# Hybrid decoder layer on one Trainium2 core: the opening's load order, cast order and count of warm-up products

## The chip, the core and the metric

The kernel runs on one core of one Trainium2 chip. The core has a matmul engine (TensorE, in the profile PE for products and PEld for weight loads), a vector engine (VectorE, DVE), a scalar engine (ScalarE, ACT), a general engine (GpSimd, POOL) and a synchronisation engine (SyncE, SP). Transfers between HBM and on-chip memory (DMAs) are issued by SP, ACT and POOL, each into a queue of its own, and move on sixteen shared DMA engines. The metric is the time of one execution on the device in microseconds (us); lower is better.

## The reference

One layer is computed for two groups of rows with shared weights: 1024 prompt rows and 64 sample rows (8 requests of 8 tokens), 1088 rows of width 1024 in all.

```python
xn = rmsnorm(x, norm1_g)
proj = xn @ w_in
q, k, v, glu_a, glu_b, gate_a, gate_b = jnp.split(proj, SPLIT_IDX, axis=-1)
...
branch_a = attn @ w_o_attn
u = glu_a * jax.nn.sigmoid(glu_b)
...
c = dwconv_valid(u_ext, conv_b_w, conv_b_bias)
branch_b = jax.nn.silu(layernorm(c, ln_b_g, ln_b_b)) @ w_pb
merged = jax.nn.sigmoid(gate_a) * branch_a + jax.nn.sigmoid(gate_b) * branch_b
h = x + merged @ w_out
up = rmsnorm(h, norm2_g) @ w_up
...
y = h + (jax.nn.silu(gate) * val) @ w_down
```

The change touches only the start of the first two lines: the norm of `x` and its product with the first pieces of `w_in`.

## The kernel before

**How a product is made.** The activations are kept transposed, channels on the partitions. Each f32 matrix is split in two: a rounded high part (a cast on ACT) and the low rest (a subtraction on DVE). `mm3` then runs three products for each 128-channel slice k: high activations with high weights (L197), low activations with high weights (L198), high activations with low weights (L199). A weight piece is 128 output channels by 1024 input channels; its 1024 columns are eight slices.

**Chunks.** The 1088 rows are taken in three chunks of 384, 384 and 320 (`CHUNKS`). `stream_side` (SIDES) runs several weight pieces side by side in a chunk: for chunk 0 the first three pieces, slice by slice, then pieces four and five one after the other; for chunk 1 two pieces side by side, then the others. So chunk 0 is 3 x 24 products for the side pieces (tiles `whi`/`wlo` twice and `whix`/`wlox`), 24 for the fourth (`whiy`/`wloy`) and 24 for the fifth (in the spare tiles `q`). Chunk 1 starts behind them with the pairs into the `aux` banks.

**The opening.** PE first runs 12 warm-up products of the tile `mean` with itself (L662); their result is not used. `norm1_load` issues the loads of chunk 0: `x_part` for slices of the rows (tile `xr`), `w_part` for columns of the three first weight pieces (tiles `wraw`, `wraw` and `u`; columns 0 to 255, 256 to 511, 512 to 1023). SP's queue takes piece one and the rows; the first and second parts of pieces two and three go through ACT's queue and POOL's. Behind those ACT loads its table and runs one small operation (`warm`, L851).

`norm1_raw` then makes the parts for chunk 0 without waiting for the norm: for each slice k, ACT scales the rows by the gain into `xh` (L283), DVE makes `xl` (L284). The weight pieces are cast in four parts of 256 columns (`W_PARTS`, two slices each), L178 on ACT and L179 on DVE. Each output row is corrected later by its own factor 1/rms, which is a column scale of the transposed output.

**The norm factors.** The squares of chunk 0 are summed by `norm1_chain` (L310 on ACT, L312 on DVE, low priority), those of chunk 1 by `norm1_squares` (L296, L294). A product with `mean` sums over the partitions (`norm1_factor`, L322), ACT takes the root (L326, tile `rows`), DVE the reciprocal and its parts (L327 to L329), six products spread the factor over the partitions (`spread`, L340), ACT copies it (L348, tile `rstd`). Chunk 1 is multiplied by its factor before its products: DVE L356 (`xr`), ACT L357 (`xh`), DVE L358 (`xl`). So chunk 1's products wait for chunk 1's factor.

**What sets the order.** Each engine runs its instructions in the order in which the program holds them. That order is made when the program is built: a scheduler takes the instructions by priority, with its own model of when each would be ready. `issue_after(x)` holds the next instruction behind x in that order; `later(...)` lowers a priority. An instruction that the scheduler thinks ready earlier can therefore be put in another place on every engine, though its line of source has not moved.

Of the kernel before, what the change touches and what calls it, by code (L numbers as in the profile page):

```python
# [8 lines left out]
AF = mybir.ActivationFunctionType  # L9
# [71 lines left out]
SQUARES_LATER = 3000  # L81
W_PARTS = 4
CONV_LATER = 1200
LN_AT = ((0, 1, 17, 36), (2, 37, 50, 80), (60, 81, 103, 134), (90, 135, 152, 183))
# [43 lines left out]
class Build:  # L128
    def __init__(self, tc, a):
        self.tc, self.nc, self.a = tc, tc.nc, a  # L130
        self.order, self.groups, self.n_in = weight_order()
        self.uid = 0
        self.agenda, self.now = [], 0

    @contextmanager
# [107 lines left out]
    def norm1_load(self, pp, c):  # L243
        o, n = CHUNKS[c]
        xr = self.t(pp, [P, KT, n], f"xr{c}")
        load = self.nc.sync.dma_start
# [10 lines left out]
        def w_part(i, x, load=load):  # L257
            z = slice(*ends[x:x + 2])
            load(self.w_raw[i][:, z], self.a["wall"][i][:, z])

        w_part(0, 0)
        x_part(0, 1)
        for x in range(2):
            for i in (1, 2):
                w_part(i, x, (self.nc.scalar, self.nc.gpsimd)[x].dma_start)
        x_part(1, 2)
# [8 lines left out]
    def norm1_raw(self, c, xr, xh, xl):  # L275
        parts = list(zip(*[self.w_parts(W_PARTS) for _ in range(SIDE)]))
        for k in range(KT):
            part = parts[k * W_PARTS // KT] if k * W_PARTS % KT == 0 else ()
            early = len(part) if k else 1
            for p in part[:early]:  # L280
                p()
            h = xh[c][:, k, :]
            self.nc.scalar.activation(h, xr[:, k, :], AF.Identity, scale=self.c("g1", k))  # L283
            self.nc.vector.scalar_tensor_tensor(xl[c][:, k, :], xr[:, k, :], self.c("g1", k), h.bitcast(F32),  # L284
                                                ALU.mult, ALU.subtract)
            for p in part[early:]:
                p()
# [340 lines left out]
    def run(self):  # L628
        nc, tc, a = self.nc, self.tc, self.a
        es = ExitStack()  # L630
        with es:
# [28 lines left out]
            ps = self.bank("mm")  # L660
            for _ in range(12):
                nc.tensor.matmul(ps[:, 0:P], self.mean, self.mean, start=True, stop=True)  # L662
# [16 lines left out]
    def phase_x(self):  # L679
# [170 lines left out]
        raw, xr[0] = self.norm1_load(p0, 0)  # L850
        nc.scalar.activation(self.warm, self.warm, AF.Sqrt)  # L851
        self.w_load()
# [1314 lines left out]
```

## Time and profile before

| what | value |
|---|---|
| time, median of 3 runs | 1641.81 us (1641.48 to 1642.1) |
| the profiled execution's own time | 1641.73 us |
| its span, first to last instruction | 1639.9 us |
| outside the span | 1.83 us |
| PE busy | 1631.1 us |
| DVE, ACT, POOL busy | 1401.3, 880.5, 262.7 us |
| bytes moved by DMA | 201.58 MB, mean 123 GB/s |

Times in the profile are microseconds from the start of the span, except where ns stands. A row of the timeline gives the start, the time taken, the engine, the line, the operation, output and input tiles (numbers of buffers left out) and how many instructions were merged; in square brackets how long the engine had been idle and what ended that. A matmul is pipelined, so the time of a row is longer than the distance to the next start; the distance between starts is what PE needs for one. Each warm-up product and each other product of plain f32 tiles stands as two records, so 12 warm-up products are 24.

### The profile page before, as it was taken

Reading aid. Unit: us, or ns where it says so; the run is one execution under the profiler, and the core shown is the slowest. Engines: PE = TensorE matmul, PEld = TensorE weight load, DVE = VectorE, ACT = ScalarE, POOL = GpSimd, SP = SyncE. Lnnn points to the kernel's source line nnn. Section 1 sums busy time; section 2 is a strip of 40 time slices with the busy share of each in tenths; the row PEclk is TensorE's granted clock in tenths of the full one; section 3 lists DMA queues with packets and bytes.
Section 4 is the critical chain, followed back from the end, with each engine's and each line's share of the span. In section 5 each row is a group of like instructions: output and inputs, shape, how many; then the busy total and the mean of one; then the engine's idle time right before and its main releaser. Section 6 shows DMA issues by size and latency. Waiting matters only on the chain.

```text
span 1639.9 us, 30209 instructions
## 1 busy us (share of the span) xinstructions
PE 1631.1 (99%) x11540; PEld 1615.2 (98%) x11540; DVE 1401.3 (85%) x2597; ACT 880.5 (54%) x1845; POOL 262.7 (16%) x549
## 2 busy tenths in 40 slices
PE   9999999999999999999999999999999999999998
PEld 9999999999999999999999999999999999999997
DVE  7899979999979996788755999988888887989867
ACT  6524277774488754676532465555555555524322
POOL 0100111222011201111102422222222111000000
PEclk9999999999999999999999999999999999999999
DMA  6221222323121356548763631344444334765413
GB/s 211 85 60 52 64 74 57 107 83 114 43 70 42 89 183 195 172 164 224 188 226 107 212 119 66 111 119 115 115 117 117 99 113 145 252 163 161 110 62 110
DMA packets 104857, 201.58 MB, mean 123 GB/s; under 512 B 25992, under 2 KB 56712, under 8 KB 104696
## 3 DMA queue, kind: packets, MB, share of 16 engines
q1 hardware_dynamic: 81384, 131.34, 26.5%
q0 software_dynamic: 22752, 67.79, 13.8%
q8 instruction: 90, 1.47, 0.4%
q10 hardware_dynamic: 576, 0.53, 0.1%
q14 instruction: 55, 0.45, 0.1%
HBM read 137.55 MB, written 64.03 MB: 123 GB/s over the span
## 4 chain that ended last, share of the span: by engine, by line
PE 87%; DVE 7%; ACT 3%; DMA 2%; issue 1%; ACTq 0%; SPq 0%; DVEq 0%; POOLq 0%
PE mm L197 20%; PE mm L198 20%; PE mm L199 20%; PE aux L199 6%; PE aux L198 6%; PE aux L197 6%; PE aux L417 1%; DVE c L531 1%; ACT ct L611 1%; PE aux L429 1%; PE aux L430 1%; PE aux L407 1%; PE aux L408 1%; DVE bt L531 1%; DMA ct<-d_c 1%
## 5 line engine op out<-in xcount | busy, mean ns | idle before, releaser
L197 PE MATMUL mm<-xh,whi 128*128 128x384 f32 (+1 forms) x904 | 301.3, 333 | 0.0
L199 PE MATMUL mm<-xh,wlo 128*128 128x384 f32 (+1 forms) x904 | 295.4, 327 | 0.0
L198 PE MATMUL mm<-xl,whi 128*128 128x384 f32 (+1 forms) x904 | 295.2, 327 | 0.1
L198 PEld LDWEIGHTS mm<-xl,whi 128*128 128x128 f32 x904 | 170.0, 188 | 1.2 <-DVE xl L284 0.4
L197 PEld LDWEIGHTS mm<-xh,whi 128*128 128x128 f32 x904 | 169.9, 188 | 0.7
L199 PEld LDWEIGHTS mm<-xh,wlo 128*128 128x128 f32 x904 | 169.7, 188 | 0.1
L1414 DVE SCALAR_TENSOR_TENSOR acc<-st,fc,acc 128x1104 f32<-128x1104 f32 x88 | 119.7, 1363 | 12.2 <-issue 6.7
L178 ACT CAST whi<-wraw 128x1024 fp32r<-128x1024 f32 (+1 forms) x62 | 59.5, 966 | 66.2 <-PE mm L198 51.7
L199 PE MATMUL mm<-th,wlo 128*128 128x272 f32 x320 | 92.4, 289 | 0.0
L197 PE MATMUL mm<-th,wlo 128*128 128x272 f32 x320 | 92.4, 289 | 0.0
L198 PE MATMUL mm<-tl,wlo 128*128 128x272 f32 x320 | 92.4, 289 | 0.0
L531 DVE SCALAR_TENSOR_TENSOR bt<-u,consts,bt 128x513 f32<-128x513 f32 x120 | 89.7, 747 | 0.7
L531 DVE SCALAR_TENSOR_TENSOR c<-sm,hsum,c 128x512 f32<-128x512 f32 x120 | 89.5, 746 | 0.7
L199 PE MATMUL mm<-mh,wlo 128*128 128x272 f32 (+4 forms) x304 | 89.2, 293 | 0.0
L531 DVE SCALAR_TENSOR_TENSOR c<-u,consts,c 128x512 f32<-128x512 f32 x112 | 83.6, 746 | 0.5
L232 ACT CAST whi<-wraw 128x512 fp32r<-128x512 f32 x76 | 47.5, 625 | 62.6 <-DVE wraw L1610 26.3
L179 DVE TENSOR_TENSOR wlo<-wraw,whi 128x1024 fp32r<-128x1024 f32 (+1 forms) x62 | 68.9, 1115 | 7.0 <-ACT whi L178 6.8
L1759 ACT COPY st<-mm 128x272 f32<-128x272 f32 (+2 forms) x132 | 43.8, 349 | 57.1 <-PE mm L199 57.1
L232 ACT CAST wlo<-wraw 128x512 fp32r<-128x512 f32 x76 | 47.4, 624 | 41.5 <-PE mm L199 18.0
L384 ACT ACTIVATE p<-p,nm 128x257 f32<-128x257 f32 (+1 forms) x128 | 62.3, 490 | 11.9 <-DVE nm L379 11.5
L1412 ACT ACTIVATE acc<-st,fc 128x1104 f32<-128x1104 f32 x44 | 57.6, 1314 | 14.5 <-DVE st L1715 11.9
L197 PE MATMUL aux<-mh,whi 128*128 128x272 f32 (+4 forms) x216 | 63.9, 296 | 0.0
(712 smaller groups left out, 5762.0 us busy)
## 6 DMA issues: line engine op xcount, KB each, us to landing
wraw<-wall SPq DMA_DIRECT2D x118, 512.0 KB, 3.9
bw<-d_b SPq DMA_DIRECT2D x42, 272.0 KB, 3.9
d_b<-gd POOLq DMA_DIRECT2D x36, 272.0 KB, 6.2
d_b<-acc POOLq DMA_DIRECT2D x24, 272.0 KB, 4.9
ar<-wdn SPq DMA_DIRECT2D x32, 192.0 KB, 3.9
d_g<-acc POOLq DMA_DIRECT2D x10, 544.0 KB, 3.8
ga<-d_ga SPq DMA_DIRECT2D x8, 544.0 KB, 5.1
ct<-d_c SPq DMA_DIRECT2D x8, 544.0 KB, 5.8
```

The source lines that it names most:

```text
L178: self.cast = self.nc.scalar.copy(h[:, z], r[:, z]).ins
L179: self.nc.vector.tensor_tensor(l[:, z], r[:, z], h[:, z].bitcast(F32), ALU.subtract)
L197: mm(ps, wh, xh, start=first, stop=False, skip_group_check=more)
L198: mm(ps, wh, xl, start=False, stop=False, skip_group_check=more)
L199: self.last_mm = mm(ps, wl, xh, start=False, stop=last, skip_group_check=more).ins
L232: self.cast = self.nc.scalar.copy(h, src).ins
L384: nc.scalar.activation(pt[:, j, lo:width + 1], pt[:, j, lo:width + 1], AF.Exp, bias=nm[:, j:j + 1], scale=-1.0, accum_out=den[:, j:j + 1])
L407: nc.tensor.matmul(ps[:, j, :], q[g][:, h, qs], kd[g][:, keys], start=True, stop=False)
L531: mac = lambda o, x, w: nc.vector.scalar_tensor_tensor(o, x, w, o, ALU.mult, ALU.add)
L1412: nc.scalar.activation(acc, st[:, 0:AW], AF.Identity, bias=fb(f), scale=fw(f, 0))
L1414: nc.vector.scalar_tensor_tensor(acc, st[:, k:k + AW], fw(f, k), acc, ALU.mult, ALU.add)
L1759: self.evicted = (add if second and n == 0 and j == 1 else op)(d, r(banks[bank, j]))
```

## The change

The load of the first row slice is issued ahead of the first weight part on SP's queue. The orders of the loads on ACT's and POOL's queues, of `warm` behind them, of ACT's scalings and of the weight casts are written out with `issue_after`. The first weight parts are now cast behind the scaling of slice 0, the scaling of slice 1 behind the first casts, and each later group of casts behind the scaling of the slice before. The warm-up has 9 products for 12.

```diff
+WARM = 9
...
-            load(self.w_raw[i][:, z], self.a["wall"][i][:, z])
-
+            return load(self.w_raw[i][:, z], self.a["wall"][i][:, z]).ins
+
+        x_part(0, 1)
         w_part(0, 0)
-        x_part(0, 1)
-        for x in range(2):
-            for i in (1, 2):
-                w_part(i, x, (self.nc.scalar, self.nc.gpsimd)[x].dma_start)
+        for x, e in enumerate((self.nc.scalar, self.nc.gpsimd)):
+            first = w_part(1, x, e.dma_start)
+            with self.tc.issue_after(first):
+                self.first_dma[x] = w_part(2, x, e.dma_start)
         x_part(1, 2)
         w_part(0, 1)
...
-            early = len(part) if k else 1
-            for p in part[:early]:
-                p()
+            early = len(part) if k else 0
+            with ExitStack() as es:
+                if early:
+                    es.enter_context(self.tc.issue_after(scaled))
+                for p in part[:early]:
+                    p()
             h = xh[c][:, k, :]
-            self.nc.scalar.activation(h, xr[:, k, :], AF.Identity, scale=self.c("g1", k))
+            with ExitStack() as es:
+                if k == 1:
+                    es.enter_context(self.tc.issue_after(self.cast))
+                scaled = self.nc.scalar.activation(h, xr[:, k, :], AF.Identity, scale=self.c("g1", k)).ins
...
-            for _ in range(12):
+            for _ in range(WARM):
                 nc.tensor.matmul(ps[:, 0:P], self.mean, self.mean, start=True, stop=True)
...
-        nc.scalar.activation(self.warm, self.warm, AF.Sqrt)
+        with tc.issue_after(self.first_dma[0]):
+            nc.scalar.activation(self.warm, self.warm, AF.Sqrt)
```

Lines move down by 2 to 10 with this: L178 becomes L180, L197 to L199 become L199 to L201, L283 becomes L292, L310 becomes L319, L322 becomes L331, L326 becomes L335, L357 becomes L366.

What it does to the order is not only in the opening. The first place is the start of PE's program: warm-up, then the first three weight pieces of slice 0 (banks `mm_256` to `mm_258`, in the changed program `mm_253` to `mm_255`). Before:

```order
L662 MATMUL mm_88<-mean_79 128x128 x12
L197 MATMUL mm_256<-xh_21_104,whi_40_163 128x384
L198 MATMUL mm_256<-xl_22_105,whi_40_163 128x384
L199 MATMUL mm_256<-xh_21_104,wlo_41_164 128x384
L197 MATMUL mm_257<-xh_21_104,whi_42_165 128x384
L198 MATMUL mm_257<-xl_22_105,whi_42_165 128x384
L199 MATMUL mm_257<-xh_21_104,wlo_43_166 128x384
L197 MATMUL mm_258<-xh_21_104,whix_167 128x384
```

And now:

```order
L671 MATMUL mm_88<-mean_79 128x128 x9
L199 MATMUL mm_253<-xh_21_101,whi_40_160 128x384
L199 MATMUL mm_254<-xh_21_101,whi_42_162 128x384
L200 MATMUL mm_253<-xl_22_102,whi_40_160 128x384
L201 MATMUL mm_253<-xh_21_101,wlo_41_161 128x384
L200 MATMUL mm_254<-xl_22_102,whi_42_162 128x384
L201 MATMUL mm_254<-xh_21_101,wlo_43_163 128x384
L199 MATMUL mm_255<-xh_21_101,whix_164 128x384
```

Three warm-up products are gone, and the second piece's first product stands one place behind the first piece's; the third piece (`whix`) still comes seventh.

The second place is ACT in the middle of chunk 0, where the casts of the third and fourth weight parts, the scaled rows and the first squares of chunk 0 (tiles `sm`, `bt`) stand. Before:

```order
L283 ACTIVATE xh_21_104<-xr_30_126,consts_77 128x384 x2
L178 CAST whi_40_163<-wraw_127 128x256
L178 CAST whi_42_165<-wraw_128 128x256
L178 CAST whix_167<-u_129 128x256
L178 CAST whi_40_163<-wraw_127 128x256
L178 CAST whi_42_165<-wraw_128 128x256
L178 CAST whix_167<-u_129 128x256
L283 ACTIVATE xh_21_104<-xr_30_126,consts_77 128x384 x2
L310 ACTIVATE sm_237<-xr_30_126 128x384
L283 ACTIVATE xh_21_104<-xr_30_126,consts_77 128x384 x2
L310 ACTIVATE bt_238<-xr_30_126 128x384
L178 CAST whiy_211<-c_145 128x512 x2
```

And now:

```order
L292 ACTIVATE xh_21_101<-xr_30_123,consts_77 128x384 x2
L180 CAST whi_40_160<-wraw_124 128x256
L180 CAST whi_42_162<-wraw_125 128x256
L180 CAST whix_164<-u_126 128x256
L319 ACTIVATE sm_234<-xr_30_123 128x384
L319 ACTIVATE bt_235<-xr_30_123 128x384
L292 ACTIVATE xh_21_101<-xr_30_123,consts_77 128x384 x2
L180 CAST whi_40_160<-wraw_124 128x256
L180 CAST whi_42_162<-wraw_125 128x256
L180 CAST whix_164<-u_126 128x256
L292 ACTIVATE xh_21_101<-xr_30_123,consts_77 128x384 x2
L180 CAST whiy_208<-c_142 128x512 x2
```

The fourth part's casts moved behind the scaling of slices 4 and 5, and both squares ahead of it.

The third place is the end of chunk 0 and the start of chunk 1. On PE, `sq` holds chunk 1's summed squares, `gt` chunk 0's; the rows between the last products of the fifth piece (`q`) and the first of chunk 1 (banks `aux_438` and `aux_439`, now `aux_435` and `aux_436`) stood so before:

```order
L199 MATMUL aux_356<-xh_21_104,q_28_123 128x384
L197 MATMUL aux_438<-xh_23_106,whi_40_163 128x384
L197 MATMUL aux_439<-xh_23_106,whi_42_165 128x384
L322 MATMUL aux_217<-mean_79,gt_240 128x1 x3
L198 MATMUL aux_438<-xl_24_107,whi_40_163 128x384
```

And now:

```order
L201 MATMUL aux_353<-xh_21_101,q_28_120 128x384
L331 MATMUL aux_214<-mean_79,gt_237 128x1 x3
L199 MATMUL aux_435<-xh_23_103,whi_40_160 128x384
L199 MATMUL aux_436<-xh_23_103,whi_42_162 128x384
L200 MATMUL aux_435<-xl_24_104,whi_40_160 128x384
```

On ACT at the same place, before (`rows_61` is chunk 1's root, `rows_68` chunk 0's, `xh_23` the high part of chunk 1):

```order
L326 ACTIVATE rows_61_363<-aux_217,consts_77 128x3
L310 ACTIVATE gt_239<-xr_30_126 128x384
L310 ACTIVATE gt_240<-xr_30_126 128x384
L348 COPY rstd_64_385<-aux_217 128x384
L357 CAST xh_23_106<-xr_35_149 128x384 x2
L326 ACTIVATE rows_68_485<-aux_217,consts_77 128x3
L357 CAST xh_23_106<-xr_35_149 128x384 x2
```

And now:

```order
L335 ACTIVATE rows_61_360<-aux_214,consts_77 128x3
L319 ACTIVATE gt_236<-xr_30_123 128x384
L319 ACTIVATE gt_237<-xr_30_123 128x384
L357 COPY rstd_64_382<-aux_214 128x384
L335 ACTIVATE rows_68_482<-aux_214,consts_77 128x3
L366 CAST xh_23_103<-xr_35_146 128x384 x4
L231 COPY u_155<-mm_253 128x384
```

Chunk 0's sum and root moved ahead of the first two casts of chunk 1 on ACT, and ahead of the first two products of chunk 1 on PE. Within the fifth piece, PE's sum of chunk 1's squares (`sq`) moved from behind its 5th product to behind its 8th, and the last five spreading products from behind its 14th to behind its 19th. POOL's order is unchanged, SP's but for the first two loads; from chunk 1 on no engine's order differs.

More of the change, by code (lines that the diff above doesn't have):

```diff
@@ L133, in __init__ @@
         self.agenda, self.now = [], 0
+        self.first_dma = [None, None]
     @contextmanager
```

## The prediction

> **What bounds the kernel now.** I read the page first, for the engine that is never free, then the chain of waits of the opening, then the timeline up to the first place where PE waits for something again.
>
> ```profile
> span 1639.9 us, 30209 instructions
> PE 1631.1 (99%) x11540; PEld 1615.2 (98%) x11540; DVE 1401.3 (85%) x2597; ACT 880.5 (54%) x1845; POOL 262.7 (16%) x549
> PE 87%; DVE 7%; ACT 3%; DMA 2%; issue 1%; ACTq 0%; SPq 0%; DVEq 0%; POOLq 0%
> ```
>
> PE is busy in 1631.1 of 1639.9 us. So a change of the opening is worth what it does to the time at which PE gets its work, and it is only kept if PE does not wait again later for something that has not come earlier too. The chain of waits, cut to the first 9 us (start, us, what):
>
> ```profile
> 1.17 0.47 ACTq L259
> 1.67 5.02 DMA u<-wall
> 6.71 0.41 ACT whix L178
> 7.12 0.53 ACT xh L283
> 7.67 0.63 DVE xl L284
> 8.34 0.44 PE mm L198
> ```
>
> This is the row to hold on to. The opening does not hang on the first row slice, nor on the first weight part, nor on the warm-up. It hangs on the first part of the THIRD weight piece (tile `u`), third load on ACT's queue: issued at 1.67, landed 5.02 us later. ACT runs in order, so the scaling of slice 1 stands behind that cast, `xl` of slice 1 behind the scaling, and at 8.34 PE gets it. The timeline around it:
>
> ```profile
> 1.05 5.36 PE L662 MATMUL mm<-mean 128*128 128x128 f32 x24 [1.05 <-DVE warm L655]
> 3.69 0.40 ACT L178 CAST whi<-wraw 128x256 fp32r<-128x256 f32 x1
> 4.86 0.62 ACT L283 ACTIVATE xh<-xr,consts 128x384 fp32r<-128x384 f32 x1 [0.76 <-DMA xr<-xT]
> 5.38 0.39 ACT L178 CAST whi<-wraw 128x256 fp32r<-128x256 f32 x1
> 6.17 0.42 PE L197 MATMUL mm<-xh,whi 128*128 128x384 f32 x1
> 6.71 0.41 ACT L178 CAST whix<-u 128x256 fp32r<-128x256 f32 x1 [0.94 <-DMA u<-wall]
> 7.31 0.34 PE L197 MATMUL mm<-xh,whix 128*128 128x384 f32 x1
> 8.34 0.19 PEld L198 LDWEIGHTS mm<-xl,whi 128*128 128x128 f32 x1 [0.42 <-DVE xl L284]
> ```
>
> The first product starts at 6.17; PE idles 0.42 us ahead of 8.34, and from there it has a product every 0.17 us until chunk 0 ends. The next waits are at chunk 1:
>
> ```profile
> 28.66 1.04 ACT L357 CAST xh<-xr 128x384 fp32r<-128x384 f32 x2 [0.69 <-DVE xr L356]
> 28.74 0.34 PE L198 MATMUL aux<-xl,q 128*128 128x384 f32 x1
> 28.91 0.34 PE L199 MATMUL aux<-xh,q 128*128 128x384 f32 x1
> 29.23 0.61 PE L197 MATMUL aux<-xh,whi 128*128 128x384 f32 x2
> 29.68 0.72 PE L322 MATMUL aux<-mean,gt 128*128 128x1 f32 x6
> 30.26 0.42 PE L198 MATMUL aux<-xl,whi 128*128 128x384 f32 x1
> 30.44 0.26 ACT L326 ACTIVATE rows<-aux,consts 128x3 f32<-128x3 f32 x1 [0.74 <-PE aux L322]
> 30.60 0.50 ACT L357 CAST xh<-xr 128x384 fp32r<-128x384 f32 x1
> 31.14 0.56 DVE L358 TENSOR_TENSOR xl<-xr,xh 128x384 fp32r<-128x384 f32 x1 [0.51 <-ACT xh L357]
> 31.61 1.67 DVE L356 SCALAR_TENSOR_TENSOR xr<-xr,consts,rstd 128x384 f32<-128x384 f32 x3
> 33.15 0.51 PE L197 MATMUL aux<-xh,whi 128*128 128x384 f32 x2
> 33.80 0.44 PE L198 MATMUL aux<-xl,whi 128*128 128x384 f32 x1
> ```
>
> Here chunk 0's root (L326, 30.44) stands on ACT between the second and third cast of chunk 1. The third cast waits for it, DVE waits for the third cast (0.51 us), and at 33.80 PE waits for the fourth slice.
>
> **The change part by part.** *Row slice ahead of weight part.* SP's first two loads change places; ACT's and POOL's keep their order. Three rows of the stretches of one us (us; busy of PE, PEld, DVE, ACT, POOL; clock; DMA share; GB/s) say what that can do:
>
> ```profile
> 4.00:5.00 1.00, 1.00 (x6) 1.00 (x6) 0.43 (x1) 0.24 (x2) 0.00 (x0) 1.00 1.04 356
> 5.00:6.00 1.00, 1.00 (x7) 1.00 (x6) 0.49 (x1) 0.77 (x2) 0.00 (x0) 1.00 1.02 302
> 6.00:7.00 1.00, 1.00 (x8) 1.00 (x8) 0.46 (x2) 0.29 (x1) 0.00 (x0) 1.00 1.01 374
> ```
>
> The DMA engines are full (share 1.0) from 4 us on, and the same bytes stand ahead of `u`. The row slice (192 KB against 128) should land near where the weight part did: 3.69 plus some 64 KB at about 300 GB/s, 0.2 us, so 3.9; both together by 4.86 as before. Then scaling 3.9 to 4.5, first cast 4.9 to 5.3, second 5.3 to 5.7; PE's first product at 5.3 for 6.17. That is 0.87 us earlier, and it buys nothing: the six products of pieces one and two run out, and PE then waits for `whix` near 7.2 as now. I take 0 for the opening. Bounds: the load of `u` may come earlier by chance or by a better turn in the shared engines, but the scaling of slice 1 then needs its own rows:
>
> ```profile
> xr<-xT SPq DMA_DIRECT2D x2, 192.0 KB, 4.8
> 1.20 0.90 SPq L247 DMA_DIRECT2D xr<-xT  x2
> ```
>
> Slices 0 and 1 are issued from 1.20 on, the second at 1.65 (half of 0.90 on), median landing 4.8: 6.45 for slice 1, against 7.02 to 7.12 when ACT begins its scaling. So at most 0.57 to 0.67 us can be gained; call it 0.6. On the other side `u` may land 0.2 us later, the time by which slice 0's larger rows delay the queue.
>
> *Nine warm-up products.* 24 records in the 5.1 us from 1.05 to 6.17 are 0.213 us each; 18 take 3.84 and end at 4.89. Now the warm-up covers the first product's wait until 6.17; without three of them PE idles 4.9 to 5.3 and again before 7.2. I take 0, with the clock as a rival below.
>
> *Order of casts and squares.* In the middle of chunk 0 ACT runs the same instructions, two squares ahead and three casts behind:
>
> ```profile
> 10.63 0.71 ACT L178 CAST whi<-wraw 128x256 fp32r<-128x256 f32 x2
> 11.55 1.12 ACT L283 ACTIVATE xh<-xr,consts 128x384 fp32r<-128x384 f32 x2
> 12.29 1.14 DVE L284 SCALAR_TENSOR_TENSOR xl<-xr,consts,xh 128x384 fp32r<-128x384 f32 x2
> 12.58 0.51 ACT L310 ACTIVATE sm<-xr 128x384 f32<-128x384 f32 x1
> 13.02 0.19 PEld L198 LDWEIGHTS mm<-xl,whi 128*128 128x128 f32 x1
> ```
>
> The three casts (0.92 us by their starts 10.63 to 11.55) give way to two squares of at most 0.51 each, so slice 4's scaling starts by 11.65 for 11.55 and its `xl`, which DVE now begins at 12.29, by 12.4, done 0.6 later at 13.0; PE wants it at 13.02. The moved casts end near 13.6, and slice 6, for which they are, is two turns of 9 products (3.1 us) behind slice 4, near 16. I take 0; the cover is the work of PE on slices 2 and 3, and if it were gone, up to one square, 0.5 us, would show.
>
> *Start of chunk 1.* This is the term that I do not cost at nothing. PE reaches the end of chunk 0 at 28.91 + 0.17 = 29.08 as now (the sum of chunk 1 and its spread only change places with products inside the fifth piece). Chunk 0's sum now comes at once, at 29.08; by the rows above the root follows 0.76 later (29.68 to 30.44), at 29.84, the next ACT instruction 0.16 after that (30.44 to 30.60), at 30.00. That next instruction is now the FIRST cast of chunk 1, which stood at 28.66. It ends at 30.5; DVE's first `xl` of 0.56 ends near 31.1; PE's first L198 of chunk 1 stands near 31.17 for 30.26, 0.91 late. What is late next: from 30.26 to 33.80 PE has 18 products and a stall. The two products at 33.15 take two turns of 0.17, so without the stall it would be at 33.50; 0.30 us of the 0.91 are eaten there, since with the new order the fourth slice's parts (DVE's second group of three 31.9 to 33.6, then 0.5) are there by 34.1 and PE comes at 34.4. Net +0.6 us. Bounds: 0, if PE reaches the end of chunk 0 earlier by the 0.6 of the opening, and +0.9, if the stall at 33.80 survives whole. Nothing later gives it back: from chunk 1 on the order is the same and PE is the bound.
>
> **Sum.** 1641.73 (the profiled execution, 0.08 under the median) + 0 (opening) + 0 (warm-up) + 0 (casts) + 0.6 (chunk 1) = 1642.3 us, 0.03% slower. A measurement of this kernel tells about 0.2%, 3.3 us, from no change; this is far inside.
>
> **The rivals.** *The early start pays* (or: the third piece lands early). If `u` lands 0.6 us sooner, PE runs 0.6 us earlier through chunk 0 and the late casts of chunk 1 cancel it: 1641.7; if the late casts are also hidden, 1641.1. For it: the load's 5.0 us is the longest of the first five, so there is room. Against it: full DMA engines, unchanged order on its queue.
>
> *The clock stays low.* For it, two rows on the pitch of 128-column products:
>
> ```profile
> 26.89 0.56 PE aux L340 x5
> ```
>
> Five spreading records in 0.56 us are 0.11 us each, against 0.213 in the warm-up, so PE ran its first 5.1 us at half speed (the stretches' clock column shows 1.00 there all the same) and rose at about 6.17, as the warm-up ended. If three products fewer and the idle pieces from 4.9 to 8.34 mean that the rise comes only after another 5.1 us of unbroken work from 8.34, PE loses half of these: 2.6 us. With the 0.6 of chunk 1: 1644.9, slower than before by 3.2. It decides if the rise is later than 8.34, since up to there PE waits anyway. Against it: PE is still busy for 3.84 us of warm-up and for some 2 of the next 3 us.
>
> The Trainium skill (TensorE: Matmul & The Clock Gate, Part 1) has a rule that speaks against this change: the clock rises after a busy window of about 3.4 us that runs free of the kernel's start, so a warm-up of 3.84 us, an estimate from our rows, holds a whole window only for some phases. By its window one missed rise costs half of 3.4, 1.7 us. The trace agrees with the half speed and the rise, 0.213 against 0.11 us; it does not show what a broken window does.
>
> *The change does nothing at all*: `consts` lands no sooner than now, so the first scaling stays near 4.9, and the root at chunk 1 falls into a gap: 1641.8.
>
> **How the numbers follow.** Forecast (1641.9 to 1643.0) 0.60; early start pays (1641.1 to 1641.8) 0.15; clock low (1643.5 to 1645.5) 0.15; nothing 0.10. Runs spread by 0.6 us. For 8 in 10 I take 1641.2 to 1643.8, which leaves out the far part of the clock's case and the tip of the early one. Over 0.2% (3.3 us) slower needs a late clock and more than the whole 0.9 at chunk 1: 0.05. Over 0.2% faster has no mechanism, since the whole idle time of the opening that can be had is 0.6: 0.02. Within 0.2%: 0.93.
>
> **What would show it.** In the changed profile: warm-up of 18 records ending near 4.9; first product near 5.3; `whix` still cast near 6.7 and L200 of slice 1 at about 8.3; the root of chunk 0 ahead of the first L366, L200 of chunk 1 near 31.2, and no stall at the fourth slice. The forecast is wrong if L200 of slice 1 comes before 8.0 or chunk 0's products show a pitch near 0.33 us behind 8.34, or if chunk 1's first cast does not wait for the root.

## The result, and the profile after

The changed kernel takes 1646.4 us (median of 9 runs, 1643.49 to 1648.22) against 1642.01 for the kernel before in the same session (9 runs, 1641.48 to 1644.72). The ratio is 1.0021, with a 95% interval of 1.0013 to 1.003. It is slower by about 4 us where 0.6 was forecast, outside the range of 1641.2 to 1643.8. The profiled execution took 1645.63 us, 3.90 above the profiled one of before:

```profile
span 1643.9 us, 30199 instructions
PE   9999999999999999999999999999999999999998
PE 54%; DVE 1%; ACT 0%; issue 0%; DVEq 0%
```

PE has no empty slice, so the loss lies in waits far smaller than a slice (41 us). They are found by pairing each of PE's products with the same product of before and reading the difference of their starts. I call it PE's delay. It is 1.30 us at slice 1 of the opening, 2.21 at 11.72, 2.03 at the end of chunk 0, 2.49 from the steady part of chunk 1 to 700 us, 3.7 behind 760 us and 3.92 at the end. Each step has its place in the trace. The opening first (timeline; the columns are those of the prediction's rows):

```profile
1.05 4.09 PE L671 MATMUL mm<-mean 128*128 128x128 f32 x18 [1.05 <-DVE warm L664]
3.53 0.60 ACT L292 ACTIVATE xh<-xr,consts 128x384 fp32r<-128x384 f32 x1
4.89 0.60 PE L199 MATMUL mm<-xh,whi 128*128 128x384 f32 x2
7.63 0.40 ACT L180 CAST whix<-u 128x256 fp32r<-128x256 f32 x1 [2.88 <-DMA u<-wall]
8.08 0.53 PE L199 MATMUL mm<-xh,whix 128*128 128x384 f32 x1 [1.90 <-ACT whix L180]
8.33 0.61 ACT L292 ACTIVATE xh<-xr,consts 128x384 fp32r<-128x384 f32 x1 [0.30 <-DMA xr<-xT]
9.65 0.69 PE L200 MATMUL mm<-xl,whi 128*128 128x384 f32 x1
10.13 0.52 PE L201 MATMUL mm<-xh,wlo 128*128 128x384 f32 x1
10.45 0.52 PE L199 MATMUL mm<-xh,whi 128*128 128x384 f32 x1
11.72 0.34 PE L200 MATMUL mm<-xl,whix 128*128 128x384 f32 x1
```

The early part came as meant: slice 0 is scaled at 3.53 (4.86 before) and PE's first product starts at 4.89 (6.17), both sooner than the forecast's 3.9 and 5.3. But the third weight piece is cast at 7.63 for 6.71, ScalarE waiting 2.88 us for its load. Slice 1's own rows are late too: issued at 1.68, they landed 6.6 us later (4.8 us before), so that the scaling of slice 1 waited another 0.30 us for them (8.33). L200 of slice 1 stands at 9.65 for 8.34. From 10.13 the starts are 0.32 us apart, not 0.17. The stretches of one us show both causes (busy shares of PE, PEld, DVE, ACT, POOL with counts; then granted clock, DMA share, GB/s):

```profile
3.00:4.00 1.00, 1.00 (x7) 1.00 (x7) 0.00 (x0) 0.99 (x3) 0.00 (x0) 1.00 1.05 212
4.00:5.00 1.00, 1.00 (x7) 1.00 (x7) 0.84 (x2) 0.75 (x3) 0.00 (x0) 1.00 0.57 147
6.00:7.00 1.00, 0.19 (x2) 0.00 (x0) 0.00 (x0) 0.00 (x0) 0.00 (x0) 1.00 0.96 291
7.00:8.00 1.00, 0.00 (x0) 0.00 (x0) 0.00 (x0) 0.37 (x1) 0.00 (x0) 1.00 1.06 385
8.00:9.00 1.00, 0.92 (x3) 0.63 (x4) 0.45 (x2) 0.70 (x3) 0.00 (x0) 0.64 1.05 402
9.00:10.00 1.00, 1.00 (x3) 0.63 (x3) 1.00 (x3) 1.00 (x4) 0.00 (x0) 0.50 1.05 398
10.00:11.00 1.00, 1.00 (x4) 1.00 (x4) 1.00 (x3) 1.00 (x3) 0.00 (x0) 0.50 1.07 395
11.00:12.00 1.00, 1.00 (x5) 1.00 (x5) 1.00 (x4) 0.84 (x4) 0.00 (x0) 0.65 1.12 400
```

In 4:5 the DMA engines moved 147 GB/s at a share of 0.57; before, 356 at 1.04. PE's clock was halved from 8.28 (0.64 in 8:9 is 0.72 us at half) to 11.70 (0.65 in 11:12), 3.42 us. In the 3.4 us ahead of that, from 4.87 to 8.28, PE had nothing for 1.90 us. The Trainium skill (TensorE: Matmul & The Clock Gate, Part 1) gives the clock's window as 3413 ns, running free of the kernel's start; that length agrees. It lets the clock fall after an idle window of about 3.4 us; here a gap of 1.90 us inside a window was enough.

At the start of chunk 1 (timeline):

```profile
30.40 0.48 ACT L357 COPY rstd<-aux 128x384 f32<-128x384 f32 x1 [1.55 <-PE aux L349]
30.91 1.68 DVE L365 SCALAR_TENSOR_TENSOR xr<-xr,consts,rstd 128x384 f32<-128x384 f32 x3 [0.91 <-ACT rstd L357]
31.12 0.72 PE L331 MATMUL aux<-mean,gt 128*128 128x1 f32 x6
31.88 0.26 ACT L335 ACTIVATE rows<-aux,consts 128x3 f32<-128x3 f32 x1 [1.00 <-PE aux L331]
32.04 1.33 ACT L366 CAST xh<-xr 128x384 fp32r<-128x384 f32 x3
32.57 1.50 DVE L367 TENSOR_TENSOR xl<-xr,xh 128x384 fp32r<-128x384 f32 x3
32.59 0.61 PE L199 MATMUL aux<-xh,whi 128*128 128x384 f32 x2 [0.75 <-ACT xh L366]
33.19 0.45 PE L200 MATMUL aux<-xl,whi 128*128 128x384 f32 x1
```

The first cast does wait for chunk 0's root, as forecast. But VectorE's first `xl` (32.57) waits for nothing: it stands behind VectorE's own three scalings, which could start only at 30.91, because the spread of chunk 1 (L349) stands 5 products later in the fifth piece than before. And far behind, near 720 us, a load of the words of `ga` (544 KB). Its issue and its use, before:

```profile
716.61 0.32 SPq L1014 DMA_DIRECT2D ga<-d_ga  x1
721.11 1.11 ACT L1015 ACTIVATE ga<-ga 128x1088 f32<-128x1088 f32 x1 [3.73 <-DMA ga<-d_ga]
```

and in the changed kernel, with waits of PE behind it:

```profile
719.21 0.32 SPq L1024 DMA_DIRECT2D ga<-d_ga  x1
725.28 1.12 ACT L1025 ACTIVATE ga<-ga 128x1088 f32<-128x1088 f32 x1 [5.30 <-DMA ga<-d_ga]
...
745.46 0.39 PE L200 MATMUL aux<-t,whi 128*128 128x272 f32 x1 [0.28 <-DVE t L235]
746.06 0.39 PE L201 MATMUL aux<-t,whi 128*128 128x272 f32 x1 [0.21 <-DVE whi L235]
749.81 0.39 PE L201 MATMUL mm<-t,wlo 128*128 128x272 f32 x1 [0.20 <-DVE wlo L235]
```

The same load is issued at the same place among the same writes of `d_ma`, yet takes 6.07 us to its use for 4.50. PE's delay grows by 0.96 us over the first two of these waits and by another 0.6 up to the third; at 761 us 0.5 is given back.

### The profile page after: what moved, and what is told of

Same layout as the page of the kernel before. It is cut to its first block, busy times and chain, and to the rows that moved or that the text cites. A ratio compares the mean times of both kernels' runs of the same rounds, so it can differ in the third digit from the quotient of the medians.

```text
span 1643.9 us, 30199 instructions
## 1 busy us (share of the span) xinstructions
PE 1632.0 (99%) x11534; PEld 1615.7 (98%) x11534; DVE 1400.8 (85%) x2597; ACT 879.9 (54%) x1845; POOL 261.9 (16%) x549
## 4 chain that ended last, share of the span: by engine, by line
PE 54%; DVE 1%; ACT 0%; issue 0%; DVEq 0%
PE mm L201 12%; PE mm L200 12%; PE mm L199 12%; PE aux L201 6%; PE aux L200 6%; PE aux L199 6%; ACT ct L620 0%; DVE t L235 0%; PE aux L1320 0%; PE mm L2025 0%; PE aux L1997 0%; DVE ct L628 0%; ACT L620 0%; DVE whi L235 0%; DVE acc L2040 0%
## 5 line engine op out<-in xcount | busy, mean ns | idle before, releaser
L199 PE MATMUL mm<-xh,whi 128*128 128x384 f32 (+1 forms) x904 | 301.6, 334 | 0.0
L201 PE MATMUL mm<-xh,wlo 128*128 128x384 f32 (+1 forms) x904 | 295.8, 327 | 0.0
L200 PE MATMUL mm<-xl,whi 128*128 128x384 f32 (+1 forms) x904 | 295.7, 327 | 0.0
L200 PEld LDWEIGHTS mm<-xl,whi 128*128 128x128 f32 x904 | 170.2, 188 | 1.1 <-DVE xl L293 0.4
L199 PEld LDWEIGHTS mm<-xh,whi 128*128 128x128 f32 x904 | 170.1, 188 | 0.9 <-ACT xh L292 0.2
L201 PEld LDWEIGHTS mm<-xh,wlo 128*128 128x128 f32 x904 | 170.0, 188 | 0.1
L180 ACT CAST whi<-wraw 128x1024 fp32r<-128x1024 f32 (+1 forms) x62 | 59.4, 966 | 63.2 <-PE mm L200 51.1
L201 PE MATMUL mm<-th,wlo 128*128 128x272 f32 x320 | 92.4, 289 | 0.0
L200 PE MATMUL mm<-tl,wlo 128*128 128x272 f32 x320 | 92.4, 289 | 0.0
L199 PE MATMUL mm<-th,wlo 128*128 128x272 f32 x320 | 92.4, 289 | 0.0
L201 PE MATMUL mm<-mh,wlo 128*128 128x272 f32 (+4 forms) x304 | 89.1, 293 | 0.0
L199 PE MATMUL aux<-mh,whi 128*128 128x272 f32 (+4 forms) x216 | 63.9, 296 | 0.0
```

The costliest lines, as they stand in the source:

```text
L180: self.cast = self.nc.scalar.copy(h[:, z], r[:, z]).ins
L199: mm(ps, wh, xh, start=first, stop=False, skip_group_check=more)
L200: mm(ps, wh, xl, start=False, stop=False, skip_group_check=more)
L201: self.last_mm = mm(ps, wl, xh, start=False, stop=last, skip_group_check=more).ins
```

## The experiments

Fifteen runs; the ratio is to the kernel before on the same chip. "Third cast" is the start of ScalarE's first cast of the third piece; the delays of PE are at chunk 0's last product and over 40 to 100 us, in the profile of that run. "Clock" counts the runs whose mean granted clock was 0.998 or less; of the kernel before, 1 run in 124 was. The mean has three digits and also holds a stretch at half clock at the end of the span (the last 2.2 us in the profile of before), so it can miss a half-clock window.

| run | third cast, us | delay, end of chunk 0 | delay, chunk 1 on | clock | median, us | ratio and interval |
|---|---|---|---|---|---|---|
| the change | 7.63 | 2.03 | 2.49 | 7 of 9 | 1646.4 | 1.0021 [1.0013, 1.003] |
| again | 7.65 | 2.03 | 2.49 | 7 of 11 | 1645.08 | 1.0019 [1.0011, 1.0028] |
| warm12 | 7.97 | 1.23 | 1.23 | 0 of 11 | 1643.2 | 1.0008 [0.9999, 1.0017] |
| weight_first | 7.04 | 0.73 | 0.76 | 0 of 11 | 1643.09 | 1.0006 [0.9997, 1.0015] |
| warm12_weight_first | 6.57 | 0.50 | 0.52 | 0 of 11 | 1642.67 | 1.0003 [0.9994, 1.0012] |
| fill | 8.60 | 2.13 | 1.53 | 0 of 11 | 1643.59 | 1.001 [1.0001, 1.0019] |
| root_behind | 8.35 | 3.00 | 3.40 | 8 of 9 | 1646.37 | 1.0024 [1.0014, 1.0033] |
| squares_back | 6.94 | 0.19 | 0.19 | 0 of 11 | 1642.58 | 1.0 [0.9991, 1.0009] |
| two_slices | 6.46 | 0.35 | -0.27 | 0 of 11 | 1641.61 | 0.9996 [0.9988, 1.0005] |
| pure_delay | 6.91 | 2.09 | 1.40 | 1 of 11 | 1645.02 | 1.0019 [1.001, 1.0028] |
| sum_back | 7.68 | 0.93 | 0.82 | 9 of 11 | 1644.79 | 1.0015 [1.0006, 1.0024] |
| long_second | 9.33 | 2.61 | 1.99 | 6 of 11 | 1644.65 | 1.0013 [1.0004, 1.0022] |
| two_slices_squares | 6.70 | 0.13 | -0.46 | 0 of 11 | 1641.86 | 0.9999 [0.999, 1.0007] |
| root_third | 7.18 | 0.44 | 0.00 | 0 of 11 | 1641.8 | 0.9997 [0.9988, 1.0006] |
| slices_root_third | 5.74 | 0.28 | -0.14 | 0 of 11 | 1642.43 | 1.0001 [0.9992, 1.001] |
| warm9_alone | 6.81 | 0.25 | 0.12 | 3 of 11 | 1642.95 | 1.0006 [0.9998, 1.0015] |

**again** is the changed kernel once more.

> The changed kernel a second time, for a second profile and for how far its runs differ. In the first profile the cast of the third piece's first part came at 7.63 us (6.71 before), the clock was granted half from 8.29 to 11.70, PE's low product of slice 1 came at 9.65 (8.34 before), and the span was 3.9 us longer. Theory A (the shorter warm-up leaves PE idle for about 2 us and the clock is granted half for one window): the half window stands in this profile too, ratio 1.0015 to 1.003. Theory B (the row slice ahead of the weight part brings the third piece late): the cast of the third piece comes at 7.3 to 7.9 again. Rival C (the late third piece was chance): the cast is back near 6.7, and the ratio is under 1.0015.

Its opening has the same steps: third cast 7.65, a half-clock stretch from 8.70, a delay of 2.49 from chunk 1 on. Slice 1's rows were in time here: its scaling stands straight behind the third cast, at 7.96, and the cast and L200 of slice 1 are both 0.94 us late. So the late piece alone is enough for most of the step; the further 0.30 us for the rows stand in the first profile only.

**warm12** undoes the count of warm-up products alone.

```diff
-WARM = 9
+WARM = 12
```

> The changed kernel with 12 warm-up products as before; the row slice stays first. With 12 the order at the start of chunk 1 is that of the kernel before. Theory A: no half window behind the opening, so 1.3 to 1.7 us of the 3.9 stay away at most, ratio 1.0005 to 1.0015. Theory B: the third piece's cast is still at 7.3 to 7.9, PE's low product of slice 1 near 9.4, 1 us late; with A and B together a ratio of 1.0005 to 1.001. Rival C: cast near 6.7 and ratio 0.9997 to 1.0003.

The third cast stays late (7.97) with a DMA share of 0.38 in 4:5, and the clock stays whole: PE's warm-up now ends near 5.9, its six products run to 7.15, and it idles 1.27 us ahead of the third piece for 1.90. The delay is 1.23 for 2.49. That also holds a change in chunk 1, since the sum and spread of chunk 1 return to their old places with the twelve products.

```profile
4.00:5.00 1.00, 1.00 (x6) 1.00 (x6) 0.81 (x2) 0.76 (x3) 0.00 (x0) 1.00 0.38 102
8.00:9.00 1.00, 0.58 (x3) 0.41 (x4) 0.50 (x2) 1.00 (x3) 0.00 (x0) 1.00 1.05 379
```

```profile
8.42 0.45 PE L199 MATMUL mm<-xh,whix 128*128 128x384 f32 x1 [1.27 <-ACT whix L180]
```

**weight_first** undoes the order of SP's first two loads alone, and **warm12_weight_first** both.

```diff
-        x_part(0, 1)
         w_part(0, 0)
+        x_part(0, 1)
```

> The changed kernel with the first weight part loaded ahead of the row slice again; 9 warm-up products stay. Theory B: the third piece's cast is back at 6.5 to 6.9, PE's low product of slice 1 near 8.4, ratio 1.0003 to 1.001 if the clock stays up. Theory A: PE still idles between 4.9 and about 7, so the half window stands here too and the ratio is 1.001 to 1.002. Rival C: the third piece's cast is late in some runs whatever the order.

> Both undone: 12 warm-up products and the weight part first; what is left of the change is the written-out order of scalings, casts and squares on ACT. PE's order is that of the kernel before. Theories A and B: ratio 0.9997 to 1.0003, third cast near 6.7, no half window behind the opening. If the order of the casts costs something by itself, as neither theory says, the ratio is above 1.0005.

The third cast comes back to 7.04 and 6.57, and the transfers fill 4:5 again (weight_first):

```profile
4.00:5.00 1.00, 1.00 (x6) 0.97 (x5) 0.00 (x0) 0.30 (x1) 0.00 (x0) 1.00 1.04 334
```

Neither has a half-clock stretch. What is left at the end of chunk 0, 0.73 and 0.50 us, is for the most part a step of PE's delay at the first two low products of slice 4: from 0.29 to 0.71 in weight_first, which is 0.3 late from slice 1 on, and from -0.12 to 0.48 in warm12_weight_first.

**fill** puts eight products of `mean` with itself between the second and third piece of slice 0 of the changed kernel, so that PE does not idle there.

```diff
+                    if c == 0 and k == 0 and i == 2:
+                        with self.tc.issue_after(self.last_mm):
+                            for _ in range(FILL):
+                                f = self.nc.tensor.matmul(p[:, 0:P], self.mean, self.mean, start=True, stop=True).ins
+                        es.enter_context(self.tc.issue_after(f))
```

> The changed kernel, 9 warm-up products and the row slice first, with 8 more products of mean with itself between the second and the third piece of slice 0; their result is not used. They keep PE at work where it idles for 1.7 to 1.9 us in the two profiles of the changed kernel. The scheduler puts chunk 0's root behind the third cast of chunk 1 in this program. Theory A (the idle time makes the half window): no half window behind 8 us, the products from 9.3 on at a pitch of 0.17, third cast still near 7.6; PE's low product of slice 1 near 9.2, and with the root moved too a ratio of 1.0005 to 1.001. Rival (the half window comes from too short a warm-up, whatever follows): a half window of 3.41 us still stands, ratio 1.0013 or more.

With the third cast at 8.60, later than in the change itself, no run of 11 shows the low clock, and it is 1.5 us above its before where again is 2.9 above its own. 0.6 of that is from chunk 1, where its sum and spread happen to stand earlier (3 and 13 products into the fifth piece) and chunk 0's root behind the third cast. So it is idle time of PE that lowers the clock, not the nine products as such.

**squares_back** holds chunk 0's early squares of warm12_weight_first behind the scalings of slices 5 and 7 and the fourth piece's casts.

```diff
+                if k < early:
+                    es.enter_context(self.tc.issue_after((self.scaled[5], self.scaled[7], self.cast4)[k]))
```

> Both of the weight part first and 12 warm-up products, and the squares of chunk 0 held behind the scalings of slices 5 and 7 and behind the fourth piece's casts. What is left of the change is the place of the fourth weight part's casts and the first cast behind the first scaling. Theory D (the squares ahead of slice 4's scaling cost 0.4 to 0.5, seen in warm12_weight_first as a step at slice 4 from -0.1 to +0.4 us): no step over 0.2 us between slices 1 and 7 against the kernel before, ratio 0.9995 to 1.0003. Rival (the step is chance of the transfers of slice 4): a step of 0.4 or more here too, or the transfers of slices 4 and 5 landing later than in the kernel before.

The step at slice 4 is gone: PE's delay is 0.22 at slice 1 and 0.20 through chunk 0. So the two squares make a step of 0.4 to 0.6 us where PE is not late by itself; at the end of chunk 0 holding them back is worth 0.3 (0.50 against 0.19).

**two_slices** loads slices 0 and 1 of warm12 as one transfer of 384 KB in first place; **two_slices_squares** holds the squares back in it too.

```diff
-        x_part(0, 1)
+        x_part(0, 2)
...
-        x_part(1, 2)
```

> The changed kernel with 12 warm-up products and row slices 0 and 1 as one load of 384 KB ahead of the first weight part; the rest as in warm12. Theory E (on each queue the third load does not start before about 4 to 4.5 us, so what stands in the first two places must be long enough to fill the time until then): the DMA share in 4 to 5 us is 0.8 or more (0.38 to 0.57 with the single slice first, 1.01 to 1.04 with the weight part first), the third piece's cast comes at 7.0 or sooner, PE's low product of slice 1 by 8.7, ratio 0.9998 to 1.0005. Rival (row data ahead of the weight part is slow in itself): share under 0.6 and third cast at 7.5 or later, ratio 1.0006 or more.

> two_slices with the squares of chunk 0 held behind the scalings of slices 5 and 7 and the fourth piece's casts. By the sum so far PE is 0.2 to 0.35 us late from slice 2 on in two_slices, which covers the squares, so nothing or up to 0.2 is gained: 1641.4 to 1641.8. If the squares still cost their 0.4, 1641.2.

The third cast stands at 6.46 and 6.70, and 4:5 is full (0.99, 344 GB/s in two_slices). Both medians are a little under the kernel before, and both intervals hold 1. Holding the squares back took 0.2 off the delay, and the medians don't tell the two apart.

**long_second** was to test how that comes about: the row slice stays first, and the first two parts of the first weight piece become one load of 256 KB in second place.

```diff
-        w_part(0, 0)
+        load(self.w_raw[0][:, 0:ends[2]], self.a["wall"][0][:, 0:ends[2]])
...
-        w_part(0, 1)
```

> Row slice first, 12 warm-ups, and the first two parts of the first weight piece as one load of 256 KB in second place. If the third load of ACT's queue is late because the first loads are over too soon (the gap at 4 to 5 us), the gap is filled (DMA share 0.9 or more at 4:5), the third piece's cast stands at 7.1 or earlier, and the median is 1642.0 to 1642.6. If it is late because a row slice, not a weight part, stands first, the share stays near 0.4 to 0.6, the cast at 7.6 to 8.6, and the median near warm12's 1643.2.

It went against both: the gap is filled for the most part, and the third cast is the latest of all, 9.33:

```profile
4.00:5.00 1.00, 1.00 (x6) 1.00 (x6) 0.62 (x1) 0.21 (x2) 0.00 (x0) 1.00 0.84 265
6.00:7.00 1.00, 1.00 (x8) 0.94 (x7) 0.14 (x1) 0.00 (x0) 0.00 (x0) 1.00 1.01 262
7.00:8.00 1.00, 0.27 (x2) 0.00 (x0) 0.00 (x0) 0.00 (x0) 0.00 (x0) 1.00 0.92 264
```

The engines move 257 to 264 GB/s from 5 to 8 us at a share near 1, but the bytes are mostly SP's. So filling the gap at 4:5 does not bring the piece earlier. The run does not single the gap out, though: the longer load also puts 128 KB more ahead of the third loads.

**root_behind** holds chunk 0's root in the changed kernel behind the second cast of chunk 1, where it stood before; **sum_back** holds PE's sum and spread of chunk 1 to near their old places (6 and 15 products into the fifth piece; before 5 and 14, changed 8 and 19).

```diff
+                    es.enter_context(tc.issue_after(edge[5]))
...
+                edge[5] = casts[1]
```

```diff
+                    if (self.now, c) in ((19, 0), (22, 0)) and self.norm_mm is not None:
+                        es.enter_context(self.tc.issue_after(self.norm_mm))
```

> The changed kernel with one thing held on ACT: the root of chunk 0 behind the second cast of chunk 1, as in the kernel before. No other instruction moves on any engine. The opening is that of the changed kernel, with the late third piece and the half window. The prediction's term (the root ahead of the casts costs 0.6): PE's distance to the kernel before grows from the end of chunk 0 to slice 3 of chunk 1 by 0 instead of the 0.3 to 0.5 in the two profiles of the changed kernel. Rival (it is already hidden by the late PE): the growth is 0.3 to 0.5 here too. The ratio, 1.0014 to 1.002, cannot tell these apart; the profile must.

> The changed kernel with PE's sum and spread of chunk 1 held to at most 6 and 15 products into the fifth piece, as before (8 and 18 in the changed kernel). If their place limits the start of chunk 1 (VectorE's three scalings start 2.2 to 2.3 us ahead of the first L200 in every profile so far), the growth of the delay from chunk 0's last product to the steady part of chunk 1, 0.47 us in the changed kernel, falls to 0.1 or less, and the time is about 0.4 under the repeat's 1645.1. If the root's place or the first cast costs it, the growth stays at 0.4 to 0.5.

The growth of the delay over the start of chunk 1 is 0.46 in the change, 0.40 with the root moved back, and -0.11 with the sum and spread moved back. In root_behind VectorE's scalings start at 31.88, only 0.21 ahead of the end of chunk 0's products, as in the change; the first `xl` comes 1.60 later and PE's L200 at 34.09:

```profile
31.88 1.68 DVE L365 SCALAR_TENSOR_TENSOR xr<-xr,consts,rstd 128x384 f32<-128x384 f32 x3 [0.91 <-ACT rstd L357]
33.48 1.49 DVE L367 TENSOR_TENSOR xl<-xr,xh 128x384 fp32r<-128x384 f32 x3
33.48 0.26 ACT L335 ACTIVATE rows<-aux,consts 128x3 f32<-128x3 f32 x1
34.09 0.45 PE L200 MATMUL aux<-xl,whi 128*128 128x384 f32 x1 [0.38 <-DVE xl L367]
```

In sum_back they start 0.90 us ahead of chunk 0's sum (29.12 against 30.02), and the first cast of chunk 1 (29.77) stands ahead of the root again:

```profile
29.12 1.68 DVE L369 SCALAR_TENSOR_TENSOR xr<-xr,consts,rstd 128x384 f32<-128x384 f32 x3
29.77 0.51 ACT L370 CAST xh<-xr 128x384 fp32r<-128x384 f32 x1 [0.69 <-DVE xr L369]
30.02 0.72 PE L335 MATMUL aux<-mean,gt 128*128 128x1 f32 x6
30.79 0.26 ACT L339 ACTIVATE rows<-aux,consts 128x3 f32<-128x3 f32 x1 [0.50 <-PE aux L335]
```

So sum_back moves the root too, by one cast, though its edit names only the sum and the spread. Taken with root_behind, where the root alone was moved and 0.40 of growth stayed, it shows that the late spread is needed for the loss; the early spread with the root still ahead of the first cast was not run. The profiled run of sum_back is one of the two of 11 without the low clock, so its delay (0.82) is less than its median says. The gain in time, 0.3 us against again, is within the intervals; the growth is read from the trace.

**root_third** moves that one instruction in the kernel before: chunk 0's root behind the third cast for behind the second. **slices_root_third** has in addition slices 0 and 1 as one load behind the first weight part.

```diff
+                    es.enter_context(tc.issue_after(edge[5]))
...
+                edge[5] = casts[2]
```

> The kernel before with one instruction moved: chunk 0's root on ScalarE behind the third cast of chunk 1 for behind the second. In the runs whose root stood there (two_slices, long_second, fill, pure_delay) the delay shrank by 0.6 to 0.7 us over the start of chunk 1, but their sums and spreads also stood 1 or 2 products earlier. If the root's place is what costs, chunk 1's steady part runs 0.6 earlier than before and the median is about 0.5 lower (1641.6); if it was the spread, 0.0 to 0.2.

> The kernel before with slices 0 and 1 as one load behind the first weight part, and the root behind the third cast. If a long load in the first two places keeps the transfers full, the third piece's cast stands at 6.4 to 6.7 and slice 1 costs nothing more, so the opening is 0 to 0.2 us earlier and the median 1641.4 to 1641.6; if the larger load delays slice 0 (its scaling starts later than 5.2 us), the opening is 0.2 later and the median 1641.8.

In root_third the delay falls by 0.44 over the start of chunk 1. VectorE no longer waits for the third cast, and the wait of before at the fourth slice (33.80) is gone:

```profile
29.10 1.57 ACT L357 CAST xh<-xr 128x384 fp32r<-128x384 f32 x3 [0.69 <-DVE xr L356]
30.05 1.49 DVE L358 TENSOR_TENSOR xl<-xr,xh 128x384 fp32r<-128x384 f32 x3
30.88 0.26 ACT L326 ACTIVATE rows<-aux,consts 128x3 f32<-128x3 f32 x1 [0.21 <-PE aux L322]
31.45 1.67 DVE L356 SCALAR_TENSOR_TENSOR xr<-xr,consts,rstd 128x384 f32<-128x384 f32 x3
```

So the root has a price of 0.44 us, but only where the spread stands early. In its profile the opening was 0.44 later by chance (third cast at 7.18 for 6.71 in a program whose opening is unchanged), so that size is also what the opening varies by. The median of root_third does not show the gain: its interval holds 1. slices_root_third gained nothing in its median either: PE is 0.3 us early at slice 1, then loses 0.5 at slice 2 and 0.1 at slice 4.

**warm9_alone** is the kernel before with nine warm-up products.

```diff
-            for _ in range(12):
+            for _ in range(9):
```

> The kernel before with nine warm-up products and the old order of loads; the sum and spread of chunk 1 then stand 2 products later and the root behind the first cast. If nine products alone make the half-clock window, the runs show a granted clock of 0.998 and the median is 1 us up, 1643.2; if it needs PE's idle time ahead of a late third piece as well, the third cast stands at 6.5 to 7.0, no window is half, and the median is 1642.0 to 1642.4.

The profile has a whole clock and a delay of 0.12, but 3 of 11 runs show a clock of 0.998, and these three are the slowest (1645.56 to 1645.93; the others 1640.94 to 1644.91). So nine products with the old loads seem enough in some runs; the profile, in which PE idled for 1.35 us, is not one of them.

**pure_delay** is the kernel before with 26 warm-up products, to make PE late and change nothing in the loads.

```diff
-            for _ in range(12):
+            for _ in range(26):
```

> The kernel before with 26 warm-up products for 12 and nothing else changed: PE's first product should move from 6.17 to about 9.15 us (28 more warm-up records at 0.107 us behind the rise of the clock), and chunk 1 by about 2.5 us, as late as in the changed kernel, but without a half-clock window and with the old orders. If lateness alone makes the later step, the load of ga near 720 us takes 5.9 us or more from its issue to the first use (as in the profiles of the changed kernel, of its repeat and of root_behind), 1 us more is lost near 742 to 757 us, and the median is about 1645.6. If the step is not from lateness, ga takes 4.3 to 4.5 us as in the other seven profiles and the median is 1642.1 + 2.5, 1644.6.

The delay in the profile was 1.40 from chunk 1 on, less than planned, since the spread also came two products earlier and chunk 0's root stood behind the third cast. `ga` took 4.44 us, so lateness alone did not slow that load in this profile. The median is 1645.02, though, 2.8 above before, and the profiled run (1643.73) was the fastest of the 11. The run does not settle the later step. The slowest of its runs (1648.27) shows the low clock, though PE has no gap in the opening of this profile; what lowered it there is not known.

## Why the prediction failed, by its steps

**The opening, taken as 0, is where it failed first.** The step that failed reads: "The DMA engines are full (share 1.0) from 4 us on, and the same bytes stand ahead of `u`", with 0.2 us as the bound on the bad side. The share was read from the old order of loads and carried over to the new one. In the new order it was 0.57 in 4:5, and `u` came late enough to move its cast by 0.92 and, with slice 1's own late rows, L200 of slice 1 by 1.31 us. The prediction had noted that the scaling of slice 1 needs these rows, but gave them the old landing too (6.45, measured near 8.3). Swapping the two loads back is enough to restore it. Over all profiles the split has no exception: with one row slice in first place the third cast stands at 7.63 to 9.33 (7 profiles), with the weight part or both slices in first place at 5.74 to 7.18 (the 10 others, before included). ACT's own queue was the same throughout. The Trainium skill (DMA: Bandwidth & Descriptors, Issuing engines are not separate DMA queues) says that transfers of all issuing engines run on the same 16 engines and interleave; that two loads on SP's queue move a third one on ACT's agrees with it. Why this order serves the third loads later is open: long_second refuted the one explanation that I had.

**The warm-up, taken as 0, failed too, by way of the clock.** The rival had the effect and the wrong shape. It feared a rise later than 8.34. The clock rose in time and fell again, after a window with PE's gap in it. Four kernels have nine products and the single slice first without filler (the change, again, root_behind, sum_back); 31 of their 40 runs show the low clock. With the gap filled it is none of 11; with twelve products and the same loads, where the gap was 1.27 us, none of 11; with twelve products and a gap of 2.52 us (long_second) 6 of 11. So the low clock goes with the length of the gap, and with the number of warm-up products only as far as that makes the gap. The price in the profiles, from slice 1 to the end of the stretch, is 0.9 us in the change (delay 1.30 to 2.21), 1.2 in again and 1.5 in root_behind, for 2.6 in the rival. Half of 3.4 would be 1.7; in the change PE waited for slice 1 until 9.65, so only the last 2.05 us of the stretch cost it about half of their length.

**The casts and squares at 0 held, for another reason.** The cover named was PE's work on slices 2 and 3; the cover that worked was that PE was late already. Without that, a step of 0.4 to 0.6 us shows, about the bound of "up to one square, 0.5 us".

**The start of chunk 1, +0.6, was near in size (0.46) by luck and wrong in its cause.** The text let the sum and spread of chunk 1 "only change places with products inside the fifth piece". That move is what costs, through `rstd` and VectorE's three scalings. With the spread that late, the root ahead of the first cast costs next to nothing on top (0.46 against 0.40), because VectorE is not ready for that cast. What the root would cost there with an early spread was not run.

**"Nothing later gives it back" held, but something later added to it.** From 700 us on the profile loses 1.4 us more. The load of `ga` goes with the first step, 0.96 us at 745 to 746 us. It took 5.65 to 6.59 us to its use in the profiles of the four kernels with nine products and the single slice first, 4.26 to 4.85 in the thirteen others; only those four have this step, and in each it is the load's time less 5.1 (0.96, 0.79, 1.44 and 0.51 us). What slows the load in just these is not shown. The further 0.6 at 749 is not shown to be the load's: weight_first has it too (0.65 to 1.25) with `ga` at 4.48. Other profiles lose time elsewhere: warm12 1.4 us at 722 on a wait for the tile `sm`, with `ga` at 4.44.

The profile's sum is 1.30 for the third piece and slice 1's rows, 0.91 for the clock, 0.46 for chunk 1, less 0.18 taken back within chunk 0: 2.49 us. With the 1.43 of later steps it is 3.92, against 3.90 measured.

Several versions have intervals that lie wholly under that of the changed kernel; two_slices and root_third have the lowest ratios. Against the kernel before they are 0.9996 [0.9988, 1.0005] and 0.9997 [0.9988, 1.0006], no difference that can be told.

## What to carry to other kernels

A DMA share read from one order of loads says nothing of another order: when two transfers at the head of a queue change places, bound the landing of every load that shares the engines, on other queues too, by what it costs if it comes last. When work is moved ahead, ask where the idle time goes that it leaves behind; a shorter warm-up in front of a longer wait can cost the clock a whole window. And when a printed order shows products moved past a sum that another engine waits for, follow that engine to its next use before calling the move free.

## What the runs showed of the hardware

Each trace records when the clock first rises; in the 17 profiles that is anywhere from 3.90 to 7.20 us. The half-clock stretches begin 3.41 us behind that rise: 8.28 behind 4.87 in the change, 8.70 behind 5.28 in again, 10.39 behind 6.98 in root_behind. In the 3.41 us ahead of the fall PE idled for 1.90, 1.73 and 1.76 us. In the profile of long_second the same count gives a step from 5.72 to 9.13 with 1.86 us of idle time, the larger part of a gap of 2.52 (7.27 to 9.79), and the clock did not fall, although 6 of its 11 runs show the low clock. So idle time of this size is near the edge, and these traces do not give the rule that decides.

A late rise can also close the gap. In the profile of sum_back the clock rose at 7.20; until then its first products ran at half speed, 0.32 us apart, so that PE idled for only 0.79 us ahead of the third piece, and the clock stayed up:

```profile
6.83 0.51 PE L202 MATMUL mm<-xh,wlo 128*128 128x384 f32 x1
8.13 0.45 PE L200 MATMUL mm<-xh,whix 128*128 128x384 f32 x1 [0.79 <-ACT whix L181]
```

Whether a gap costs a window thus differs from run to run of one program. The opening itself varies too: the third cast stood at 6.71, 7.18, 6.81 and 6.91 in four profiles of programs whose opening loads are those of the kernel before.
